# Where in a partition the operands of the matmuls begin: offsets at multiples of 256 and 512 bytes in a hybrid encoder

## The chip, the cores and the metric

The kernel runs on one core of a Trainium2 chip. The metric is the time of one execution on the device, in microseconds. The kernel before was run three times, 2456.8 to 2458.05 us, median 2456.95 us.

## The reference

The trunk has two layers over 16 meta tokens and 256 tokens (272 rows, 2048 features), all in float32. Each layer is a token mixer and a SwiGLU, each behind an RMS norm and added to the residual:

```
h = concatenate(meta, x)                                   # [272, 2048]
layer 0: h += fft2(norm(h), tokens and 256 features).real @ fnet_w_out
         h += (silu(u @ w_gate) * (u @ w_up)) @ w_down     # u = norm(h), 5632 hidden features
layer 1: z, xbc, dt = norm(h) @ ssd_w_in                   # bidirectional state space (SSD) mixer
         y = ssd(silu(conv5(xbc)), dt) forward + backward, 64 heads in 8 groups
         h += group_norm(y * silu(z)) @ ssd_w_out
         h += swiglu(norm(h))
out = norm(h)[16:]
```

## The kernel before

The residual `hT` is held feature-major: 128 partitions, 16 feature blocks, 272 tokens. Every large product is made of three matmuls (`mm3`, L103 to L106): each float32 operand is split in a high and a low part of type float32r, and high·high, high·low and low·high are summed in PSUM. The operands of the activations are `gh`/`gl` (of the normed residual, made by `norm_block`, L142), `hh`/`hl` (of the hidden layer of a SwiGLU), `yh`/`yl` (of the SSD mixer's output) and `fh`/`fl` (of the Fourier mixer). The weights come in units of 1 MB by DMA into `w` (3 buffers); ACT copies each half to `wh` (L97), DVE subtracts to get `wl` (L98), four buffers each. TensorE takes them in this order:

- Fourier mixer, then `fnet_w_out`: weights `wh`/`wl` are the stationary operand, `fh`/`fl` the moving one, 272 columns (to 154 us).
- SwiGLU of layer 0, in pieces of 8 feature blocks: gate and up (`gemm_in`, L115) move `gh`/`gl`, 272 columns; down (`down0`) moves `hh`/`hl`, 272 columns (to 935 us).
- SSD mixer in 8 groups: products with `w_in` move `gh`/`gl` (272 or 258 columns); the gate z turns the roles round and moves `wh`/`wl`, 512 columns, against stationary `gh`/`gl`; small float32 products within a group; `w_out` (`out_group`, L571) moves `yh`/`yl`, 256 columns (to 1706 us).
- Last SwiGLU on the 256 tokens alone: gate and up move `gh`/`gl`, 256 columns; down (`down1`) moves `wh`/`wl`, 512 columns, against stationary `hh`/`hl`.

In `gemm_in` and `down0` each block k of the contraction gives six matmuls in a row that share k: two column blocks j, three products each.

Tiles are placed one behind the other, at multiples of 32 bytes, in the order in which the pools and the tiles in them are made. In the built program `gh` begins at byte 33920 of a partition, `gl` at 51328, `wh` at 98560 and `wl` at 114944 (four buffers of 4096 bytes each), `hh` and `hl` of layer 0 at 134592 and 152000 (8704 bytes each buffer), `yh` and `yl` at 203488 and 211680, `hh` and `hl` of the last SwiGLU at 161280 and 177664. A row (one feature block) of `gh`, `fh` and of layer 0's `hh` has 272 words, 1088 bytes; of `yh` and of the last SwiGLU's `hh` 256 words, 1024 bytes. Modulo 256 the weights thus begin at 0, slices of 128 columns too; rows of 1088 bytes take the offsets 0, 64, 128, 192 by turns; `yh` and `yl` have 224 in every row, the last SwiGLU's `hh` and `hl` 0. In the last SwiGLU gate and up read tokens 16 to 271 of rows of 272.

The schedule is the order in which the code is written, moved by priorities of the splitting (L96); waits come from the tiles' uses.

Of the kernel before, what the change touches and what calls it, by code (L numbers as in the profile page):

```python
# [19 lines left out]
P = 128  # L20
D = 2048
NB = D // P            # 16 feature blocks
NM = 16                # meta tokens
KM = 64 + NM           # rows that hold them three times, from 0, 32 and 64
S = 256
L = NM + S             # 272
FG = 8                 # fnet groups
FD = D // FG           # 256
NK = L // 2 + 1        # 137 token frequencies
# [4 lines left out]
HG = H // G            # heads per group  # L34
NST = 128
DFF = 5632
NF = DFF // P          # 44
EPS = 1e-6
CA = (NM, NM + P)      # token chunk A
CB = (NM + P, L)       # token chunk B  # L40
XC, BC, CC = 0, DI, DI + G * NST      # columns of x, B, C
NRAW, NSP = 3, 4       # buffers: weights as they come (8 KiB a partition), their parts (4 + 4 KiB)
RUN = 1024             # words of a weight block that a partition holds one after the other
HC = 8                 # feature blocks of a piece of the SwiGLU hidden layer
# [4 lines left out]
def encoder(ctx: ExitStack, tc: tile.TileContext, I, out):  # L49
# [4 lines left out]
    wpool = ctx.enter_context(tc.tile_pool(name="wpool", bufs=1))  # L54
    pmm = ctx.enter_context(tc.tile_pool(name="pmm", bufs=4, space=PSUM))
# [16 lines left out]
    rbc = const.tile([P, L], F32, name="rbc")  # L72
    ssq = const.tile([P, L], F32, name="ssq")
# [10 lines left out]
    def weights(src, k0, nk, c0, ncol):  # L84
        """Unit of a weight matrix (see blocks), rows (k0..k0+nk)*128, columns c0..c0+ncol, as (high, low) parts."""
# [16 lines left out]
    def mm3(ps, lhs, rhs, start, stop):  # L102
        """ps (+)= lhs.T @ rhs of operands split as (high, low)."""  # L103
        PE.matmul(ps, lhs[0], rhs[0], start=start, stop=False)  # L104
        PE.matmul(ps, lhs[0], rhs[1], start=False, stop=False)  # L105
        PE.matmul(ps, lhs[1], rhs[0], start=False, stop=stop)  # L106
# [4 lines left out]

    def gsl(k, a, b=L):
        return gh[:, k, a:b], gl[:, k, a:b]

    def gemm_in(src, c0, lo):  # L115
        """Two blocks of 128 columns of norm(h) @ src, feature-major, over the tokens lo.. ."""
        n = L - lo
        pss = [mmtile(), mmtile()]
        for k0 in (0, 8):
            u = weights(src, k0, 8, c0, 256)  # L120
            for k in range(8):
                for j in range(2):
                    mm3(pss[j][:, :n], wsl(u, k, j * P), gsl(k0 + k, lo), k0 + k == 0, k0 + k == NB - 1)
        return pss

    def rsqrt(pool, x, n, tag):
        """1/sqrt(x) of [P, n]: bit-level seed and three Newton steps."""
# [12 lines left out]
    npool = ctx.enter_context(tc.tile_pool(name="npool", bufs=1))  # L140

    def norm_block(b, wcol, lo):  # L142
        """Block b of the residual is final: operand of the next product and sum of squares."""
        SC.activation(gh[:, b, lo:], hT[:, b, lo:], AF.Identity, bias=0.0, scale=wcol)
        V.scalar_tensor_tensor(out=gl[:, b, lo:], in0=hT[:, b, lo:], scalar=wcol,
                               in1=gh[:, b, lo:].bitcast(F32), op0=ALU.mult, op1=ALU.subtract)
# [7 lines left out]
    def norm_scale(lo):  # L154
        """rbc = 1/rms of every token, the same on all partitions."""
        ps = tptile()
        PE.matmul(ps[:, : L - lo], ones, ssq[:, lo:], start=True, stop=True)
        x = npool.tile([P, L], F32, tag="nx", name="nx")
# [16 lines left out]
    # =====================================================================  # L175
    # Fourier mixer
    # =====================================================================
    with ExitStack() as fx:
# [3 lines left out]
        tok = early.tile([P, 2, L], F32, name="tok")  # L182
        tokM = early.tile([KM, L], F32, name="tokM")
# [3 lines left out]
        tm3 = early.tile([KM, L], F32R, name="tm3")  # L187
        th = early.tile([P, 2, L], F32R, name="th")
        tl = early.tile([P, 2, L], F32R, name="tl")
# [4 lines left out]
        # parts of x where the spectrum comes later  # L194
# [49 lines left out]
        def table(c, r):  # L244
            """Token table of chunk c scaled by 1/rms."""
# [4 lines left out]
        with tc.manual_schedule():  # L250
            # residual, feature-major, parts of x, mean squares of the tokens
# [37 lines left out]
            # meta tokens: three products of parts in one, rows 0.. high high, 32.. high low, 64.. low high  # L289
# [8 lines left out]
            # token transform: cosines 0..NK-1, sines 1..NK-2  # L298
# [20 lines left out]
        # feature transform; operands in F32R have an even number of columns, so one more than is used  # L319
# [37 lines left out]
    # =====================================================================  # L357
    # SwiGLU, the hidden layer in pieces of HC feature blocks
    # =====================================================================
    def swiglu(layer, lo, tmp, pieces, down):  # L360
# [3 lines left out]
        for nf in pieces:  # L364
            hh = tmp.tile([P, HC, n], F32R, tag="hh", name="hh", bufs=2)
            hl = tmp.tile([P, HC, n], F32R, tag="hl", name="hl", bufs=2)
# [43 lines left out]
    # =====================================================================  # L410
    # bidirectional SSD mixer
    # =====================================================================
    with ExitStack() as fx:
# [7 lines left out]
        rtok = sc0.tile([P, 2], F32, name="rtok")  # L421
# [3 lines left out]
        sp = fx.enter_context(tc.tile_pool(name="ssd", bufs=1))  # L425

# [9 lines left out]
        # The products with the large weights are emitted in slots; the rest of a group follows its slots at a  # L436
        # distance, so that the tensor engine has a product to go on with meanwhile.
# [12 lines left out]
        def step_sizes():  # L450
# [6 lines left out]
            # 1/rms of the tokens of chunks A and B, one token a partition  # L457
# [14 lines left out]
            # softplus(v) = max(v, 0) + log1p(exp(-|v|)), log1p(t) = 2 atanh(t / (2 + t))  # L472
# [16 lines left out]
            # prefix sums within the chunks: inclusive forward, exclusive backward  # L489
# [42 lines left out]
        def conv(ps, blk, lo, dst):  # L532
            """Depthwise conv over the tokens lo.. of the 128 channels of block blk, then silu."""
            n = L - lo
            u = sp.tile([P, L], F32, tag="cu", name="cu", bufs=2)
            V.tensor_tensor(out=u[:, :n], in0=ps[:, :n], in1=rbc[:, lo:], op=ALU.mult)
            a = sp.tile([P, L], F32, tag="ca", name="ca", bufs=2)
# [10 lines left out]
        def to_tokens(src, dst, dstM):  # L548
            """[128 channels, 272 tokens] -> [tokens, 128 channels] of the chunks A, B and of the meta tokens."""
# [7 lines left out]
        def out_group(gi, q, yh, yl):  # L557
            """Residual += y @ w_out over the channels of group gi, columns 512q.. ."""
# [12 lines left out]
        def group_rest(gi, cT, btok, btokM, xt, xtM, zs, cb):  # L571
            """All of a group after its products with w_in."""
# [5 lines left out]
            def kernels(c):  # L578
                """Within chunk c: sum over both directions of exp(decay) dt B.C, [source, head, target]."""
# [11 lines left out]
            # weighted inputs  # L591
# [24 lines left out]
            sums = sp.tile([P, 2], F32, tag="sums", name="sums", bufs=2)  # L616
            gated = []

            def mix(c):
                """y of chunk c: other chunks' parts, this chunk's part, skip connection; then the gate."""  # L620
# [31 lines left out]
            def norm():  # L652
                """Grouped norm, back to feature-major."""
                V.tensor_scalar(out=sums, in0=sums, scalar1=1.0 / 512, scalar2=EPS, op0=ALU.mult, op1=ALU.add)
                rg = rsqrt(sp, sums, 2, "rg")
                later(1, lambda: back(rg))
# [29 lines left out]
        def decays(gi):  # L686
            """Cumulated log decays of a group's heads on all partitions."""
# [7 lines left out]
        def drop(gi):  # L695
            """The half that a direction doesn't see decays to nothing."""
# [11 lines left out]
        for gi in range(G):  # L708
            if gi % 2 == 0:
# [1 line left out]
                bT = sp.tile([P, 2, L], F32, tag="bT", name="bT", bufs=2)  # L711
                cT = sp.tile([P, 2, S + 2], F32, tag="cT", name="cT", bufs=1)
# [11 lines left out]
            # x of the group  # L724
# [4 lines left out]
            def source_target(gj=gi % 2, cb=cb, bT=bT, cT=cT):  # L729
                """B.C of all sources and targets within the chunks."""  # L730
# [7 lines left out]
            for h2 in range(2):  # L738
                for j, ps in enumerate(gemm_in(I["w_xbc"], XC + gi * 512 + h2 * 256, 0)):
                    bj = 2 * h2 + j  # L740
                    xs = sp.tile([P, L], F32, tag="xs", name="xs", bufs=4)
# [5 lines left out]
            # silu(z) of the group  # L747
# [27 lines left out]
    # =====================================================================  # L775
    # last SwiGLU, final norm
    # =====================================================================
    with ExitStack() as fx:
# [4 lines left out]
        sums = tmp.tile([P, 2, 4], F32, name="fsums")  # L783
        sqj = tmp.tile([P, 512], F32, name="fsq")
        ms = tmp.tile([P, 2], F32, name="fms")

        def down1(f0, nf, hh, hl):
            if f0 == 0:
                # residual, one token a partition
# [59 lines left out]
def tables():  # L849
    """Constants that follow from the shapes."""  # L850
# [20 lines left out]
def blocks(w, ncol):  # L871
    """[.., rows, columns] in blocks [rows of blocks, columns of blocks, 128, (k c)]: RUN words, that is RUN / ncol
    rows 128 apart of ncol columns, one after the other."""
# [6 lines left out]
def arrays_of(inputs):  # L880
    """The matrices in blocks, the per-feature vectors one after the other in rows of 128, the tables."""
# [28 lines left out]
```

## Time and profile before

| | |
|---|---|
| median of the runs | 2456.95 us |
| span of the profiled execution, first to last instruction | 2455.8 us |
| TensorE busy | 2428.0 us, 99% |
| VectorE busy | 1484.5 us, 60% |
| ScalarE busy | 1214.1 us, 49% |
| GpSimd busy | 406.6 us, 17% |
| HBM read over the span | 433.66 MB, 177 GB/s |

The profiled execution is told by its span; what lies around it is the 1.15 us to the median. A row of a group of instructions gives its line, engine, operation, output and inputs, shapes, count, busy time and the mean of one. Matmuls overlap, so that a mean duration is more than what one matmul takes of the span.

### The profile page before, as it was taken

What the parts mean: (1) busy time and instruction counts of PE and PEld (TensorE: products, weight loads), DVE (VectorE), ACT (ScalarE), POOL (GpSimd) and SP (SyncE); (2) the same over time, 40 slices, a digit from 0 to 9 for tenths busy, and PEclk for the clock granted to TensorE, in tenths of its full rate; (3) what the DMA queues carried; (4) which work ended last, traced back from release to release, by engine and by line L of the source; (5) the groups of instructions that cost most, each with busy time, mean ns of one, the idle gap of its engine ahead of it and who ended that gap; (6) DMA issues with size and microseconds to landing.
All of it is one profiled execution on the core that took longest, in us unless ns stands there. A gap on an engine that the chain in (4) does not pass through costs nothing.

```text
span 2455.8 us, 42928 instructions
## 1 busy us (share of the span) xinstructions
PE 2428.0 (99%) x17958; PEld 2316.9 (94%) x17958; DVE 1484.5 (60%) x2020; ACT 1214.1 (49%) x1784; POOL 406.6 (17%) x361
## 2 busy tenths in 40 slices
PE   8999999999999999999999999999999999999998
PEld 8999999999999999888989989989999998989887
DVE  7564545545454568778668668668554555555556
ACT  6444333343434346878557558445444343444434
POOL 3111111010101112232221221112211010102000
PEclk9999999999999999999999999999999999999999
DMA  5555555555555555655455555454555555555553
GB/s 164 175 178 179 173 173 176 181 175 172 175 181 177 172 173 175 213 175 186 164 179 193 177 172 184 159 172 157 201 187 178 189 189 189 189 190 188 189 192 134
DMA packets 115506, 438.66 MB, mean 179 GB/s; under 512 B 7360, under 2 KB 8080, under 8 KB 115136
## 3 DMA queue, kind: packets, MB, share of 16 engines
q1 hardware_dynamic: 110336, 417.86, 50.4%
q0 software_dynamic: 4832, 17.99, 2.3%
q8 instruction: 141, 2.31, 0.4%
q14 instruction: 53, 0.43, 0.0%
q10 hardware_dynamic: 144, 0.07, 0.0%
HBM read 433.66 MB, written 2.23 MB: 177 GB/s over the span
## 4 chain that ended last, share of the span: by engine, by line
PE 89%; DVE 3%; DMA 3%; issue 2%; ACT 2%; POOL 1%; SPq 0%; DVEq 0%; ACTq 0%; POOLq 0%
PE mm L105 29%; PE mm L106 28%; PE mm L104 28%; DMA pb<-scr 2%; DVE wl L98 1%; PE tp L642 1%; ACT wh L97 1%; DVE ca L544 1%; PE tp L626 0%; PE tp L665 0%; DMA w<-fnet_w_out 0%; POOL pb L701 0%; ACT pb L584 0%; DMA x<-x 0%; PE tp L608 0%
## 5 line engine op out<-in xcount | busy, mean ns | idle before, releaser
L98 DVE TENSOR_TENSOR wl<-w,wh 128x1024 fp32r<-128x1024 f32 x786 | 970.0, 1236 | 840.7 <-ACT wh L97 832.7
L97 ACT CAST wh<-w 128x1024 fp32r<-128x1024 f32 x786 | 822.8, 1048 | 1096.6 <-PE mm L105 809.2
L105 PE MATMUL mm<-gl,wh 128*128 128x272 f32 (+2 forms) x3600 | 1026.0, 285 | 0.0
L106 PE MATMUL mm<-gh,wl 128*128 128x272 f32 (+2 forms) x3600 | 1022.3, 284 | 0.5 <-DVE wl L98 0.5
L104 PE MATMUL mm<-gh,wh 128*128 128x272 f32 (+2 forms) x3600 | 1022.4, 284 | 0.1
L104 PEld LDWEIGHTS mm<-gh,wh 128*128 128x128 f32 x3600 | 678.2, 188 | 1.1 <-issue 0.5
L106 PEld LDWEIGHTS mm<-gh,wl 128*128 128x128 f32 x3600 | 676.3, 188 | 0.9 <-DVE wl L98 0.7
L105 PEld LDWEIGHTS mm<-gl,wh 128*128 128x128 f32 x3600 | 676.1, 188 | 0.8 <-issue 0.5
L378 POOL TENSOR_TENSOR s<-s,rbc 128x272 f32<-128x272 f32 (+1 forms) x88 | 96.4, 1113 | 816.4 <-ACT s L377 816.4
L105 PE MATMUL mm<-hl,wh 128*128 128x272 f32 x704 | 203.7, 289 | 0.0
L106 PE MATMUL mm<-hh,wl 128*128 128x272 f32 x704 | 202.7, 288 | 0.0
L104 PE MATMUL mm<-hh,wh 128*128 128x272 f32 x704 | 200.9, 285 | 0.0
L385 POOL TENSOR_TENSOR hl<-t,hh 128x272 fp32r<-128x272 f32 (+1 forms) x88 | 97.0, 1121 | 397.1 <-ACT hh L384 397.1
L104 PE MATMUL mm<-yh,wh 128*128 128x256 f32 x512 | 146.5, 288 | 3.8 <-DVE hT L567 3.3
L105 PE MATMUL mm<-yl,wh 128*128 128x256 f32 x512 | 143.6, 281 | 0.5 <-DVE yl L671 0.5
L106 PE MATMUL mm<-yh,wl 128*128 128x256 f32 x512 | 143.5, 281 | 0.0
L105 PE MATMUL mm<-wl,hh 128*128 128x512 f32 x352 | 137.1, 390 | 0.0
L104 PE MATMUL mm<-wh,hh 128*128 128x512 f32 x352 | 137.0, 389 | 0.0
L106 PE MATMUL mm<-wh,hl 128*128 128x512 f32 x352 | 137.0, 389 | 0.0
L104 PEld LDWEIGHTS mm<-hh,wh 128*128 128x128 f32 x704 | 132.9, 189 | 0.0
L106 PEld LDWEIGHTS mm<-hh,wl 128*128 128x128 f32 x704 | 132.3, 188 | 0.0
L105 PEld LDWEIGHTS mm<-hl,wh 128*128 128x128 f32 x704 | 132.1, 188 | 0.0
(279 smaller groups left out, 2858.5 us busy)
## 6 DMA issues: line engine op xcount, KB each, us to landing
w<-ffn_w_gate SPq DMA_DIRECT2D x88, 1024.0 KB, 5.1
w<-ffn_w_up SPq DMA_DIRECT2D x88, 1024.0 KB, 5.1
w<-w_down SPq DMA_DIRECT2D x80, 1024.0 KB, 5.1
w<-w_xbc SPq DMA_DIRECT2D x48, 1024.0 KB, 5.2
w<-w_z SPq DMA_DIRECT2D x32, 1024.0 KB, 5.3
w<-ssd_w_out SPq DMA_DIRECT2D x32, 1024.0 KB, 5.1
w<-fnet_w_out SPq DMA_DIRECT2D x16, 1024.0 KB, 5.1
pb<-scr POOLq DMA_DIRECT2D x32, 512.0 KB, 5.6
```

The lines of the kernel that those rows point to most:

```text
L97: SC.copy(wh, w[:, ks, :])
L98: V.tensor_tensor(out=wl, in0=w[:, ks, :], in1=wh.bitcast(F32), op=ALU.subtract)
L104: PE.matmul(ps, lhs[0], rhs[0], start=start, stop=False)
L105: PE.matmul(ps, lhs[0], rhs[1], start=False, stop=False)
L106: PE.matmul(ps, lhs[1], rhs[0], start=False, stop=stop)
L378: GP.tensor_tensor(out=s1, in0=s1, in1=rbc[:, lo:], op=ALU.mult)
L385: GP.tensor_tensor(out=hl[:, f, :], in0=t2, in1=hh[:, f, :].bitcast(F32), op=ALU.subtract)
L544: V.scalar_tensor_tensor(out=a[:, o0:o1], in0=u[:, i0 : i0 + o1 - o0], scalar=w(j), in1=a[:, o0:o1], op0=ALU.mult, op1=ALU.add)
L642: PE.matmul(py[:, e * HD : (e + 1) * HD], kern[c][:, e, :], xt[:, c, e * HD : (e + 1) * HD], start=True, stop=True)
```

## The change

Tiles are placed otherwise, and two of them are laid out otherwise:

- A pad of 384 bytes ahead of `hT` brings `hT`, `gh`, `gl`, `ident`, `ones` and `cols` to multiples of 512 bytes; `rbc` and `ssq` go to the norm's pool, which now stands behind the weights' pool and has its own pad. `w`, `wh` and `wl` so begin at multiples of 512 too (`wh` at 96768).
- In the pools of the Fourier mixer and the SSD mixer the tiles that TensorE reads most come first; those of 272 columns or of a few words go to the end or to a pool of their own (`so`).
- `hh`/`hl` of layer 0's SwiGLU get rows of 320 words (1280 bytes), of which 272 are used. All their rows, and all of `yh`/`yl`, begin at 0 modulo 256.
- For tokens 16 to 271 (the last SwiGLU's input) `norm_block` writes and `gemm_in` reads a compact view of `gh`/`gl`: 16 rows of 256 words from the tile's start, 1024 bytes apart.
- `nx` shares the buffer of `sq`; the final norm's small tiles share one of 512 bytes.

The instructions and their order are the same on all five engines, but for the names of tiles.

```diff
+    npool = ctx.enter_context(tc.tile_pool(name="npool", bufs=1))
...
+    const.tile([P, LINE - 32], F32, name="pad")
     hT = const.tile([P, NB, L], F32, name="hT")
     gh = const.tile([P, NB, L], F32R, name="gh")
     gl = const.tile([P, NB, L], F32R, name="gl")
...
-    rbc = const.tile([P, L], F32, name="rbc")
-    ssq = const.tile([P, L], F32, name="ssq")
...
+    gh1, gl1 = (x.rearrange("p b t -> p (b t)")[:, : NB * S].rearrange("p (b t) -> p b t", t=S) for x in (gh, gl))
+
     def gsl(k, a, b=L):
+        if (a, b) == (NM, L):
+            return gh1[:, k, :], gl1[:, k, :]
         return gh[:, k, a:b], gl[:, k, a:b]
...
+    rbc = npool.tile([P, L], F32, name="rbc")
+    ssq = npool.tile([P, L], F32, name="ssq")
+
+    npool.tile([P, L], F32, tag="sq", name="sq", bufs=1)
+    npool.tile([P, L], I32, tag="nyi", name="nyi")
+    npool.tile([P, LINE // 2], F32, name="pad2")
...
     def norm_block(b, wcol, lo):
-        SC.activation(gh[:, b, lo:], hT[:, b, lo:], AF.Identity, bias=0.0, scale=wcol)
-        V.scalar_tensor_tensor(out=gl[:, b, lo:], in0=hT[:, b, lo:], scalar=wcol,
-                               in1=gh[:, b, lo:].bitcast(F32), op0=ALU.mult, op1=ALU.subtract)
+        high, low = gsl(b, lo)
+        SC.activation(high, hT[:, b, lo:], AF.Identity, bias=0.0, scale=wcol)
+        V.scalar_tensor_tensor(out=low, in0=hT[:, b, lo:], scalar=wcol,
+                               in1=high.bitcast(F32), op0=ALU.mult, op1=ALU.subtract)
...
-        x = npool.tile([P, L], F32, tag="nx", name="nx")
+        x = npool.tile([P, L], F32, tag="sq", name="nx", bufs=1)
...
-            hh = tmp.tile([P, HC, n], F32R, tag="hh", name="hh", bufs=2)
-            hl = tmp.tile([P, HC, n], F32R, tag="hl", name="hl", bufs=2)
+            hh = tmp.tile([P, HC, n + -n % 64], F32R, tag="hh", name="hh", bufs=2)[:, :, :n]
+            hl = tmp.tile([P, HC, n + -n % 64], F32R, tag="hl", name="hl", bufs=2)[:, :, :n]
...
         sp = fx.enter_context(tc.tile_pool(name="ssd", bufs=1))
+        so = fx.enter_context(tc.tile_pool(name="ssdo", bufs=1))
...
-            u = sp.tile([P, L], F32, tag="cu", name="cu", bufs=2)
+            u = so.tile([P, L], F32, tag="cu", name="cu", bufs=2)
...
-                bT = sp.tile([P, 2, L], F32, tag="bT", name="bT", bufs=2)
-                cT = sp.tile([P, 2, S + 2], F32, tag="cT", name="cT", bufs=1)
+                bT = so.tile([P, 2, L], F32, tag="bT", name="bT", bufs=2)
+                cT = so.tile([P, 2, S + 2], F32, tag="cT", name="cT", bufs=1)
```

## Rows read from the trace of the kernel before

**Rows 1.** The page's head and parts 1 and 2: span, busy time, granted clock

```profile
span 2455.8 us, 42928 instructions
PE 2428.0 (99%) x17958; PEld 2316.9 (94%) x17958; DVE 1484.5 (60%) x2020; ACT 1214.1 (49%) x1784; POOL 406.6 (17%) x361
PEclk9999999999999999999999999999999999999999
```

**Rows 2.** The page's part 4, the chain by line

```profile
PE mm L105 29%; PE mm L106 28%; PE mm L104 28%; DMA pb<-scr 2%; DVE wl L98 1%; PE tp L642 1%; ACT wh L97 1%; DVE ca L544 1%; PE tp L626 0%; PE tp L665 0%; DMA w<-fnet_w_out 0%; POOL pb L701 0%; ACT pb L584 0%; DMA x<-x 0%; PE tp L608 0%
```

**Rows 3.** Who TensorE waited for: us in total, times, longest us

```profile
PE tp L225 <- DMA ident<-c_ident: 5.2, 1, 5.2
PE mm L104 <- DVE hT L567: 3.3, 4, 1.6
```

**Rows 4.** Groups of instructions by shape: count, busy us, mean ns, idle before

```profile
L104 PE MATMUL mm<-gh,wh 128*128 128x272 f32 x2064 | 591.2, 287 | 0.0
L104 PE MATMUL mm<-gh,wh 128*128 128x256 f32 x1408 | 394.5, 280 | 0.1
L105 PE MATMUL mm<-hl,wh 128*128 128x272 f32 x704 | 203.7, 289 | 0.0
L104 PE MATMUL mm<-yh,wh 128*128 128x256 f32 x512 | 146.5, 288 | 3.8 <-DVE hT L567 3.3 <-ACT yh L670 0.5
L104 PE MATMUL mm<-wh,hh 128*128 128x512 f32 x352 | 137.0, 389 | 0.0
L104 PE MATMUL mm<-wh,gh 128*128 128x512 f32 x256 | 101.6, 397 | 0.0
```

**Rows 5.** Stretches of one kind of matmul, busy us and count by engine

```profile
core 0: us, PE busy (x) PEld busy (x) DVE busy (x) ACT busy (x) POOL busy (x), PEclk, DMA share, GB/s
160.00:280.00 120.00, 120.00 (x963) 120.00 (x962) 60.11 (x68) 50.41 (x63) 24.49 (x22) 1.00 0.49 166
841.00:931.00 90.00, 90.00 (x722) 90.00 (x721) 57.10 (x73) 41.46 (x57) 11.96 (x14) 1.00 0.53 176
1000.00:1016.00 16.00, 16.00 (x71) 12.99 (x70) 13.13 (x14) 14.23 (x27) 1.44 (x2) 1.00 0.61 206
1684.00:1696.00 12.00, 12.00 (x104) 12.00 (x103) 10.38 (x19) 8.11 (x17) 6.16 (x5) 1.00 0.40 145
1720.00:1880.00 160.00, 160.00 (x1370) 160.00 (x1369) 84.91 (x99) 69.23 (x87) 32.57 (x30) 1.00 0.57 190
1893.00:1933.00 40.00, 40.00 (x178) 33.15 (x177) 21.18 (x21) 15.82 (x15) 0.00 (x0) 1.00 0.49 162
```

**Rows 6.** TensorE in order of time: start us, duration, a run at offset 0

```profile
start us, us, engine line op out<-in xcount [idle before <-releaser]
2002.20 0.27 PE L105 MATMUL mm<-gl,wh 128*128 128x256 f32 x1
2002.32 0.28 PE L106 MATMUL mm<-gh,wl 128*128 128x256 f32 x1
2002.43 0.28 PE L104 MATMUL mm<-gh,wh 128*128 128x256 f32 x1
2002.55 0.28 PE L105 MATMUL mm<-gl,wh 128*128 128x256 f32 x1
2002.67 0.28 PE L106 MATMUL mm<-gh,wl 128*128 128x256 f32 x1
```

**Rows 7.** The same, end of a run at offset 192

```profile
2004.44 0.28 PE L106 MATMUL mm<-gh,wl 128*128 128x256 f32 x1
2004.55 0.28 PE L104 MATMUL mm<-gh,wh 128*128 128x256 f32 x1
2004.66 0.28 PE L105 MATMUL mm<-gl,wh 128*128 128x256 f32 x1
2004.78 0.28 PE L106 MATMUL mm<-gh,wl 128*128 128x256 f32 x1
```

**Rows 8.** Groups by shape again, the SSD mixer's largest small product

```profile
L642 PEld LDWEIGHTS tp<-xt,pb 128*128 128x128 f32 x256 | 31.1, 192 | 7.7 <-issue 6.9 <-PE mm L106 0.5 <-DVE cu L536 0.2
```

More of the change, by code (lines that the diff above doesn't have):

```diff
@@ L43 @@
 RUN = 1024
+LINE = 128
 HC = 8
@@ L138, in rsqrt @@
         return y
-    npool = ctx.enter_context(tc.tile_pool(name="npool", bufs=1))
+    rbc = npool.tile([P, L], F32, name="rbc")
[3 more added lines that the diff above has]
+    npool.tile([P, LINE // 2], F32, name="pad2")
     def norm_block(b, wcol, lo):
-        SC.activation(gh[:, b, lo:], hT[:, b, lo:], AF.Identity, bias=0.0, scale=wcol)
-        V.scalar_tensor_tensor(out=gl[:, b, lo:], in0=hT[:, b, lo:], scalar=wcol,
-                               in1=gh[:, b, lo:].bitcast(F32), op0=ALU.mult, op1=ALU.subtract)
+        high, low = gsl(b, lo)
+        SC.activation(high, hT[:, b, lo:], AF.Identity, bias=0.0, scale=wcol)
+        V.scalar_tensor_tensor(out=low, in0=hT[:, b, lo:], scalar=wcol,
+                               in1=high.bitcast(F32), op0=ALU.mult, op1=ALU.subtract)
         if b == 0:
@@ L181, in encoder @@
         xm = early.tile([KM, D], F32, name="xm")
-        tok = early.tile([P, 2, L], F32, name="tok")
-        tokM = early.tile([KM, L], F32, name="tokM")
         feat = early.tile([P, 2, 2, FD], F32, name="feat")
@@ L186, in encoder @@
         xm3 = early.tile([KM, D], F32R, name="xm3")
-        tm3 = early.tile([KM, L], F32R, name="tm3")
-        th = early.tile([P, 2, L], F32R, name="th")
-        tl = early.tile([P, 2, L], F32R, name="tl")
         fth = early.tile([P, 2, 2, FD], F32R, name="fth")
@@ L193, in encoder @@
         fl = early.tile([P, NB, L], F32R, name="fl")
+        tok = early.tile([P, 2, L], F32, name="tok")
+        tokM = early.tile([KM, L], F32, name="tokM")
+        tm3 = early.tile([KM, L], F32R, name="tm3")
+        th = early.tile([P, 2, L], F32R, name="th")
+        tl = early.tile([P, 2, L], F32R, name="tl")
         xh = fh.rearrange("p b t -> p (b t)")[:, : 2 * D].rearrange("p (c d) -> p c d", c=2)
@@ L420, in encoder @@
         dsk = sc0.tile([P, H], F32, name="dsk")
-        rtok = sc0.tile([P, 2], F32, name="rtok")
+        rtok = sc0.tile([P, 2 + 2 * 8], F32, name="rtok")[:, 0:2]
         scr = dram.tile([P, 2 * P], F32, name="scr")
@@ L534, in conv @@
             n = L - lo
-            u = sp.tile([P, L], F32, tag="cu", name="cu", bufs=2)
+            u = so.tile([P, L], F32, tag="cu", name="cu", bufs=2)
             V.tensor_tensor(out=u[:, :n], in0=ps[:, :n], in1=rbc[:, lo:], op=ALU.mult)
-            a = sp.tile([P, L], F32, tag="ca", name="ca", bufs=2)
+            a = so.tile([P, L], F32, tag="ca", name="ca", bufs=2)
             def w(j):
@@ L614, in states @@
                 SC.copy(st[:, 2, :], ps)
-            sums = sp.tile([P, 2], F32, tag="sums", name="sums", bufs=2)
+            sums = so.tile([P, 2], F32, tag="sums", name="sums", bufs=2)
             gated = []
@@ L654, in norm @@
                 V.tensor_scalar(out=sums, in0=sums, scalar1=1.0 / 512, scalar2=EPS, op0=ALU.mult, op1=ALU.add)
-                rg = rsqrt(sp, sums, 2, "rg")
+                rg = rsqrt(so, sums, 2, "rg")
                 later(1, lambda: back(rg))
@@ L740, in encoder @@
                     bj = 2 * h2 + j
-                    xs = sp.tile([P, L], F32, tag="xs", name="xs", bufs=4)
+                    xs = so.tile([P, L], F32, tag="xs", name="xs", bufs=4)
                     conv(ps, 4 * gi + bj, 0, xs)
@@ L782, in encoder @@
         GP.dma_start(fw, I["norm_final_w"].partition_broadcast(P))
-        sums = tmp.tile([P, 2, 4], F32, name="fsums")
         sqj = tmp.tile([P, 512], F32, name="fsq")
-        ms = tmp.tile([P, 2], F32, name="fms")
+        small = tmp.tile([P, LINE], F32, name="fsmall")
+        sums = small[:, 0:8].rearrange("p (c q) -> p c q", c=2)
+        ms = small[:, 8:10]
         def down1(f0, nf, hh, hl):
```

## The prediction

> **What bounds the kernel now.** I read the page's first two parts, then the chain, then TensorE's waits, then the groups of matmuls, and last a table of stretches. TensorE is busy 2428.0 of 2455.8 us, at the full granted clock from end to end [rows 1], and 85% of the chain are the three matmul lines L104 to L106 [rows 2]. What TensorE waits for is small: the longest waits are 5.2 us for the first transfer and 3.3 us behind L567 [rows 3]. So only the pace of the matmuls can move the time by much. The order of instructions doesn't move: on all five engines the changed program has the same rows in the same order, names aside, and two waits fewer, both on DVE. The change is one of addresses alone.
>
> The pace is not read from the duration of one matmul (280 to 397 ns, [rows 4]), since matmuls overlap; it is the distance from start to start. In a stretch that holds one kind only, that is (length of the stretch + one duration) / count. From [rows 5], with durations from [rows 4]:
> - gate and up of layer 0, 272 columns: (120 + 0.287) / 963 = 124.9 ns
> - down of layer 0, 272 columns: (90 + 0.289) / 722 = 125.05 ns
> - the gate z, 512 columns: (16 + 0.397) / 71 = 230.9 ns
> - `w_out`, 256 columns: (12 + 0.288) / 104 = 118.2 ns
> - gate and up of the last SwiGLU, 256 columns: (160 + 0.280) / 1370 = 117.0 ns
> - down of the last SwiGLU, 512 columns: (40 + 0.389) / 178 = 226.9 ns
>
> Two of these have the same shape and the full clock [rows 5], and differ: 230.9 against 226.9 ns at 512 columns. Their moving operand is the same buffer (`wh`, `wl`); the stationary one is `gh`/`gl` with rows of 1088 bytes in the first, `hh`/`hl` with rows of 1024 bytes in the second. In both, the load of the next weights runs beside the matmul (PEld is busy in the same stretch, [rows 5]). So where the two reads lie to one another costs TensorE time. At 226.9 / 512 = 0.443 ns a column the even stretch is also the quickest per column of the six: the others come to 0.451 to 0.462.
>
> I count offsets modulo 256 bytes: in the even stretch the moving tiles begin at 256 and the stationary ones at 0 modulo 512, and it is even all the same. That 0 against 0, which it will be afterwards, runs alike is an assumption; if not, 1056 matmuls times 4.0 ns = +4.2 us.
>
> **The change part by part.** Modulo 256 nothing changes where rows stay 1088 bytes apart, since four rows in turn take the offsets 0, 64, 128 and 192 wherever the tile begins: Fourier output, gate and up of layer 0, all products with `w_in`, z. I cost these at 0. Three families change.
>
> Gate and up of the last SwiGLU (3 x 1408 = 4224 matmuls): the compact rows of 1024 bytes put every moving operand at offset 0 against weights at 0, where they cycle through four offsets now. At the rate of the even stretch one takes 256 x 0.443 = 113.4 ns, so 4224 x (117.0 - 113.4) = -15.2 us. Each k of a unit makes six matmuls in a row at one offset, and k is counted from the unit's start. The trace has this pace at 256 columns already: at the end of the run of six with offset 192 the starts go 2004.44, 2004.55, 2004.66, 2004.78, that is 0.34 / 3 = 113 ns [rows 7]. Against it stands the run of six with offset 0, from 2002.20 to 2002.67 0.47 / 4 = 117.5 ns, and its last two steps are 0.12 each [rows 6]. A run of six may still carry the offsets before it, the even stretch has hundreds in a row; so I take 113.4, and keep 120 as the upper bound.
>
> `w_out` (3 x 512 = 1536 matmuls): `yh` and `yl` lie at 224 modulo 256 now, all rows alike, and will lie at 0. A single offset is thus not enough for the good pace (118.2 ns). The same 113.4 gives 1536 x (113.4 - 118.2) = -7.4 us; its row has only 104 matmuls, so this term is good to about 1.5 us.
>
> Down of layer 0 (3 x 704 = 2112 matmuls): rows of 1280 instead of 1088 bytes, all at offset 0, but each operand has 1088 bytes, so the next one doesn't begin where this one ends, as it does with 1024. No row shows this. Bounds: the even rate gives 272 x 0.443 = 120.5 ns, 2112 x -4.55 = -9.6 us; the 120 ns of above, 6.6 over the even 113.4, put on 120.5 gives 127.1, +4.3 us. I take 0, between them and at the row of today.
>
> The small products of the SSD mixer (`xt`, `pb`, `xw`, `st`, `dg`): the largest group is L642, 256 weight loads of 192 ns, 31.1 us in all [rows 8]; a tenth of that either way would be 3 us, I take 0. On ACT, DVE and POOL the same operations stand with the same element counts; moved buffers make no new wait, and where the last SwiGLU now overlies `yh` and `yl`, its first writes come behind products that follow the readers on TensorE anyway. That a quicker TensorE is fed: in the stretch of gate and up DVE is busy 84.91, ACT 69.23 of 160 us and the DMA engines 0.57 [rows 5], so 3% more pace has its cover; without it the 15.2 us would not come.
>
> Sum: -15.2 - 7.4 + 0 = -22.6 us. The profiled span is 2455.8 us and the median of the runs 2456.95, so 1.15 us lie around the span and are not touched: 2456.95 - 22.6 = 2434.4 us (2434.35).
>
> A sentence of the Trainium skill speaks against all this: TensorE: Matmul & The Clock Gate (section Step-by-step: what each phase is for) says that TensorE has two independent read ports, so that loading the next weights takes no read bandwidth from the running matmul, and SBUF — State Buffer (Operand start alignment) calls where an operand starts a matter of legality, not of speed, though it timed nothing. By that the two stretches of 512 columns would run alike; they differ by 4.0 ns, so the trace does not agree. That page of the Trainium skill gives for matmuls back to back (section Back-to-back issue gap) columns / 2.4 + 2.5 ns, which would be 215.8 ns at 512 and 109.2 at 256 columns; no stretch here reaches it, the measured pace goes into the sum.
>
> **The rivals.**
> 1. A fixed offset of 0 is no better than the mix. For it: the run at offset 0 makes 117.5 ns [rows 6], and `w_out` with a fixed offset makes 118.2. Against it: the even 512. Price: 4224 x (117.5 - 117.0) - 1536 x (118.2 - 117.5) = +2.1 - 1.1 = +1.0 us, 2458; by 118.2 for both +5.1 us, 2462; a pace of 116 gives -4.2 - 3.4 = -7.6, 2449.4.
> 2. It is slower: at 256 columns a matmul and the load beside it meet in the same place at every step, because both begin at 0 and nothing shifts them. At 512 the second half of a matmul has no load beside it, in which it can get clear; at 256 there is no such half. For it: the run at offset 0 gets slower towards its end, 0.12 and 0.12 [rows 6]. Against it: the same pair of offsets in the even stretch. Price at 120 ns: 4224 x 3.0 + 1536 x 1.8 + 4.3 = 12.7 + 2.8 + 4.3 = +19.8 us, 2476.8. It decides from the point where the pace at offset 0 is over 117.3 ns: there the two large terms cancel.
> 3. Offsets don't matter, and the 4 ns at 512 columns come from the other work beside them (z has ACT busy 14.23 of 16 us, the even stretch 15.82 of 40): 2457. The two ports of the Trainium skill (TensorE: Matmul & The Clock Gate, section Step-by-step: what each phase is for) would make this of it.
>
> **How the numbers follow.** A measurement of this kernel can tell about 0.2%, 4.9 us, from no change. Forecast 0.48: 2434.4, its own range 2420 to 2443 (down of layer 0 at its lower or upper bound, with 3 us of the small products and 1.5 us of `w_out`). Rival 1 0.25, spread over 2449 to 2463: 0.06 faster, 0.12 same, 0.07 slower. Rival 2 0.20. Rival 3 0.07, same. Together 0.54 faster, 0.19 same, 0.27 slower. The range for 8 in 10 goes from 2422 to 2474: nearly all of the forecast, rivals 1 and 3 whole, the milder part of rival 2.
>
> **What would show it.** In the changed profile the stretch of gate and up in the last SwiGLU has one start each 113.4 ns (1413 in 160 us instead of 1370), `w_out` likewise, down of layer 0 between 120.5 and 127, and gate and up of layer 0 still 124.9, z 230.9, the last down 226.9. The waits of TensorE stay as short as now. If gate and up keep 117 or go to 120, the forecast is wrong at its first term; if a family that I left at 0 moves, offsets count otherwise than modulo 256; if waits of TensorE for L98 grow, the quicker pace was not fed.

## The result, and the profile after

The changed kernel takes 2472.51 us (median; 2471.03 to 2473.42) against 2457.4 for the kernel before in the same comparison (2456.8 to 2458.05): ratio 1.0061, 95% interval 1.0047 to 1.0076. It is slower by 15.1 us. The forecast was 2434.4 us, so its sign was wrong; the slower rival's price was 2476.8.

The head of the page after shows that hardly anything but TensorE's own pace has changed [rows 1]:

```profile
span 2470.8 us, 42926 instructions
PE 2443.7 (99%) x17958; PEld 2333.9 (94%) x17958; DVE 1484.2 (60%) x2020; ACT 1213.7 (49%) x1784; POOL 404.6 (16%) x361
PEclk9999999999999999999999999999999999999999
```

The span grew by 15.0 us and TensorE's busy time by 15.7, with the same 17958 matmuls. Away from the two ends of the span the granted clock is the same but for one place: from 1106.7 to 1110.1 us it was 0.50, the lower of its two levels (1.2 GHz), after TensorE had waited 1.70 us for L569. The sixteen matmuls there took 3.39 us against 2.07 before, so about 1.3 of the 15.0 us are the clock's; none of the families that the change touches ran then. The busy times of DVE, ACT and POOL moved by 2 us or less. The chain still runs over the three matmul lines (L105 to L107 now, [rows 2]), and TensorE's waits are as short as before [rows 3]:

```profile
PE mm L106 30%; PE mm L107 29%; PE mm L105 29%; DVE wl L99 1%; PE tp L656 1%; DMA pb<-scr 1%; ACT wh L98 1%; PE tp L679 0%; PE tp L640 0%; DMA w<-fnet_w_out 0%; DVE ca L558 0%; PE tp L622 0%; PE tp L619 0%; ACT pb L598 0%; PE tp L627 0%
```

```profile
PE mm L105 <- DVE hT L581: 3.9, 4, 1.9
```

The stretches that answer to [rows 5], of the kernel after (later stages begin up to 15 us later, so the windows are shifted). The columns are the window in us, then busy us and, in brackets, the count of instructions on each engine, TensorE's granted clock, the DMA share, and GB/s:

```profile
160.00:280.00 120.00, 120.00 (x962) 120.00 (x962) 58.81 (x65) 50.33 (x64) 24.55 (x22) 1.00 0.48 163
842.00:932.00 90.00, 90.00 (x720) 90.00 (x719) 58.48 (x74) 41.40 (x59) 11.59 (x13) 1.00 0.51 175
1000.00:1016.00 16.00, 16.00 (x71) 12.99 (x70) 12.79 (x12) 13.65 (x25) 3.31 (x3) 1.00 0.63 222
1178.00:1188.00 10.00, 10.00 (x86) 10.00 (x85) 4.77 (x9) 3.15 (x3) 0.00 (x0) 1.00 0.43 136
1724.00:1884.00 160.00, 160.00 (x1335) 160.00 (x1335) 82.73 (x94) 67.74 (x86) 30.71 (x29) 1.00 0.55 185
1900.00:1940.00 40.00, 40.00 (x178) 33.15 (x177) 21.02 (x21) 15.82 (x15) 0.00 (x0) 1.00 0.47 163
```

By the prediction's formula (stretch plus one duration, over the count), gate and up of the last SwiGLU, the fifth row, went from 1370 starts to 1335: (160 + 0.283) / 1335 = 120.06 ns instead of 117.0. Layer 0's gate and up (125.0), z (230.9) and the last down (226.9) stand where they stood, and layer 0's down moved little (90.29 / 720 = 125.4). The fourth row, `w_out`, is short: 10.28 / 86 = 119.5, good to about 1%. Within the stretch of gate and up, matmul follows matmul (columns: start us, duration):

```profile
2002.00 0.28 PE L105 MATMUL mm<-gh,wh 128*128 128x256 f32 x1
2002.12 0.28 PE L106 MATMUL mm<-gl,wh 128*128 128x256 f32 x1
2002.24 0.28 PE L107 MATMUL mm<-gh,wl 128*128 128x256 f32 x1
2002.36 0.28 PE L105 MATMUL mm<-gh,wh 128*128 128x256 f32 x1
```

Each step is 0.12 us. The last two steps of [rows 6] were the same 0.12; [rows 7] had 0.34 / 3 = 0.113.

For exact sums I added the distances from each matmul's start to the next one's in both traces, family by family:

| family | matmuls | before, us | after, us | difference |
|---|---|---|---|---|
| gate and up, last SwiGLU, 256 columns | 4224 | 494.4 | 507.1 | +12.7 |
| `w_out`, 256 columns, its waits included | 1536 | 190.9 | 193.7 | +2.8 |
| down of layer 0, 272 columns | 2112 | 264.0 | 264.7 | +0.7 |
| gate and up of layer 0 and products with `w_in`, 272 columns | 6192 | 781.1 | 781.4 | +0.3 |
| last down, 512 columns | 1056 | 239.8 | 239.8 | 0 |
| z, 512 columns | 768 | 181.1 | 180.7 | -0.4 |
| small products of the SSD mixer | 734 | 116.0 | 115.2 | -0.8 |

The first three rows are +16.2 us and the others take about 1 back (the 1.3 us of the slower clock are in the fourth and the last row). The largest row, +12.7 us, is the family that reads the compact view.

### The profile page after: what moved, and what is told of

It reads as the page before. It is cut to its first block, busy times and chain, and to the rows that moved or that the text cites. A ratio compares the mean times of both kernels' runs of the same rounds, so it can differ in the third digit from the quotient of the medians.

```text
span 2470.8 us, 42926 instructions
## 1 busy us (share of the span) xinstructions
PE 2443.7 (99%) x17958; PEld 2333.9 (94%) x17958; DVE 1484.2 (60%) x2020; ACT 1213.7 (49%) x1784; POOL 404.6 (16%) x361
## 4 chain that ended last, share of the span: by engine, by line
PE 92%; DVE 3%; ACT 1%; DMA 1%; issue 1%; POOL 0%; SPq 0%; DVEq 0%; ACTq 0%; POOLq 0%
PE mm L106 30%; PE mm L107 29%; PE mm L105 29%; DVE wl L99 1%; PE tp L656 1%; DMA pb<-scr 1%; ACT wh L98 1%; PE tp L679 0%; PE tp L640 0%; DMA w<-fnet_w_out 0%; DVE ca L558 0%; PE tp L622 0%; PE tp L619 0%; ACT pb L598 0%; PE tp L627 0%
## 5 line engine op out<-in xcount | busy, mean ns | idle before, releaser
L107 PE MATMUL mm<-gh,wl 128*128 128x272 f32 (+2 forms) x3600 | 1029.6, 286 | 0.5 <-DVE wl L99 0.5
L105 PE MATMUL mm<-gh,wh 128*128 128x272 f32 (+2 forms) x3600 | 1027.1, 285 | 0.0
L105 PEld LDWEIGHTS mm<-gh,wh 128*128 128x128 f32 x3600 | 684.4, 190 | 1.1 <-issue 0.7
L107 PEld LDWEIGHTS mm<-gh,wl 128*128 128x128 f32 x3600 | 682.4, 190 | 0.9 <-DVE wl L99 0.7
L107 PE MATMUL mm<-hh,wl 128*128 128x272 f32 x704 | 202.4, 288 | 0.0
L105 PE MATMUL mm<-hh,wh 128*128 128x272 f32 x704 | 202.4, 287 | 0.0
L105 PE MATMUL mm<-yh,wh 128*128 128x256 f32 x512 | 147.4, 290 | 4.4 <-DVE hT L581 3.9
L107 PE MATMUL mm<-yh,wl 128*128 128x256 f32 x512 | 144.5, 283 | 0.0
L105 PE MATMUL mm<-wh,hh 128*128 128x512 f32 x352 | 137.1, 389 | 0.0
L107 PE MATMUL mm<-wh,hl 128*128 128x512 f32 x352 | 136.9, 389 | 0.0
L105 PEld LDWEIGHTS mm<-hh,wh 128*128 128x128 f32 x704 | 132.4, 188 | 0.0
L107 PEld LDWEIGHTS mm<-hh,wl 128*128 128x128 f32 x704 | 132.3, 188 | 0.0
```

## The experiments

All numbers on offsets below are modulo 256 bytes. "192 on 0" means that the moving operand begins at 192 and the stationary one at 0. In the changed kernel everything in the three families is 0 on 0. The kernels differ from the changed one in addresses alone.

**Another single offset.** All three families at 192 on 0:

```diff
-    ... [:, : NB * S] ... for x in (gh, gl))
+    ... [:, 48 : 48 + NB * S] ... for x in (gh, gl))
+            if gi == 0:
+                sp.tile([P, 48], F32, name="ypad")
...
-            hh = ... [:, :, :n]
+            hh = ... [:, :, 48 : 48 + n]      # layer 0; hl alike
```

> The changed kernel, but the compact gh and gl, yh and yl, and the rows of layer 0's hh and hl all begin at 192 modulo 256 instead of 0; the weights stay at 0. Theory 1 (the offset of the moving operand to the weights sets the pace, and 0 is a bad one at 256 columns): gate and up of the last SwiGLU and w_out go at 113.4 ns a matmul, as the end of the run at offset 192 in the kernel before did, instead of 120.0; that is (4224 + 1536) x -6.6 = -38 us against the changed kernel, about 2434.5 us; the 272 columns of layer 0's down between 120.5 and 125. Theory 2 (rows that never shift against the weights are bad at any offset): 118 to 120 ns stay, 2465 to 2473 us. Theory 3 (it is not the offset but the layout in rows of 1024 bytes): 120 ns stay in gate and up, 2472 us.

Measured: 2452.68 us, ratio to the kernel before 0.9978 (0.9969 to 0.9987). Its trace has two paces at the same shape and the same offsets. The rows are down of layer 0, two stretches of `w_out`, and gate and up:

```profile
842.00:928.00 86.00, 86.00 (x699) 86.00 (x698) 56.32 (x71) 40.65 (x58) 11.47 (x13) 1.00 0.50 173
1159.00:1168.00 9.00, 9.00 (x82) 9.00 (x81) 7.84 (x15) 8.05 (x19) 5.60 (x5) 1.00 0.43 142
1172.00:1182.00 10.00, 10.00 (x87) 10.00 (x86) 5.16 (x9) 2.92 (x4) 0.27 (x1) 1.00 0.42 125
1712.00:1872.00 160.00, 160.00 (x1361) 160.00 (x1360) 83.94 (x96) 69.07 (x87) 32.60 (x30) 1.00 0.55 188
```

`w_out` runs at 9.28 / 82 = 113 ns in one stretch and at 10.28 / 87 = 118 in the next. From start to start (the mean distance of neighbouring starts, from the second tenth of a stretch on) it is 113.3 and 117.8, each held to the end of the stretch. The six stretches behind the mixer's 512-column products (`xw`, `btok`) have 117.8, six behind 128-column ones (`dg`, `yg` or `ident`, `xs`) 113.3. Gate and up have 113.3 in their first 96 matmuls and 160.28 / 1361 = 117.8 in all that follow. So the offset matters (120 became 117.8), down of layer 0 gained 1.9 ns (123.45), and the 113 ns that the forecast counted on exist. But the offset alone does not give them. The program may not either: nine of this kernel's ten runs lie between 2451.31 and 2453.81 us, one took 2445.89. The first long stretch of gate and up, 1440 matmuls, at 113.3 instead of 117.8 would take 6.5 us less (an estimate from the two paces); that run has no trace, so this is not shown.

**The compact view taken back**, the rest of the change kept:

```diff
     def gsl(k, a, b=L):
-        if (a, b) == (NM, L):
-            return gh1[:, k, :], gl1[:, k, :]
         return gh[:, k, a:b], gl[:, k, a:b]
```

> The changed kernel without the compact view: in the last SwiGLU gh and gl keep rows of 1088 bytes, everything else as changed. Theories 1, 2 and 3 alike: gate and up go back from 120.0 to 117.0 ns, 4224 x -3.0 = -12.7 us, about 2460 us, and what is left of the loss (2 to 3 us) is w_out, still at 120 ns. If gate and up stay at 120 the other moved tiles did it, and all three theories fall.

Measured: 2459.3 us, ratio 1.0006 (0.9997 to 1.0016), no difference that can be told. Gate and up are back at 117.0 (160.28 / 1371 = 116.9), `w_out` is still at 120.0 from start to start:

```profile
1724.00:1884.00 160.00, 160.00 (x1371) 160.00 (x1370) 83.64 (x94) 69.19 (x87) 32.54 (x30) 1.00 0.55 190
```

The kernel is 13.2 us quicker than the changed one. That settles which edit costs the time: the view, which fixes at 0 what had cycled through four offsets.

**Sweeps over offsets**, one run each. The same edits as in the first experiment, with 64 and 224 for gate and up, 128 and 32 for `w_out`, and another offset in each piece of layer 0's hidden layer:

> The changed kernel with other offsets, to read paces by stretch: compact gh and gl at 64, yh and yl at 128, the six pieces of layer 0's hh and hl at 32, 32, 64, 96, 128 and 160 bytes. Theory 1: gate and up about 117.6 ns (the run at 64 of the kernel before), w_out about 117 (the run at 128), the pieces at 272 columns differ from each other by several ns between 120.5 and 128. Theory 2: all at 256 columns 118 to 120 ns, all pieces alike. Theory 3: gate and up at 120, w_out at 118 to 120.

> As the sweep before, with the compact gh and gl at 224, yh and yl at 32, the six pieces of layer 0's hh and hl at 0, 16, 48, 80, 112 and 144 bytes. Theory 1: gate and up at 118.2 ns, which is what w_out had in the kernel before at the same offset of 224 (one offset, one pace, whichever the tile); w_out at 32 has no row, anything from 113 to 121; piece 0 at 125.3 as in the changed kernel. Theory 2: 118 to 120 everywhere. Theory 3: gate and up stay at 120.

Measured: 2463.73 and 2459.59 us. Gate and up at 64 and at 224, the first run and then the second:

```profile
1724.00:1884.00 160.00, 160.00 (x1361) 160.00 (x1360) 83.94 (x96) 69.06 (x87) 32.59 (x30) 1.00 0.55 187
```

```profile
1724.00:1884.00 160.00, 160.00 (x1354) 160.00 (x1353) 80.19 (x86) 68.28 (x87) 32.52 (x30) 1.00 0.55 186
```

With the paces from start to start, over both runs, the first one, and for `w_out` at 160 the run entered from 0 below:

| moving offset, on weights at 0 | 256 columns, ns | 272 columns, ns |
|---|---|---|
| 0 | 120.0 | 125.3 |
| 16 / 32 / 48 | - / 116.7 / - | 124.4 / 125.7 / 125.0 |
| 64 | 117.8 | 126.7 |
| 80 / 96 / 112 | - | 125.0 / 126.7 / 126.7 |
| 128 | 118.7 or 120.0 | 126.7 |
| 144 / 160 | - / 117.3 or 118.7 | 124.4 / 123.4 |
| 192 | 117.8 or 113.3 | 123.3 |
| 224 | 118.3 | - |
| four in turn | 117.0 | 125.0 |

Each offset has its pace or pair of paces, 0 is the slowest at 256 columns (128 comes to the same 120.0 in five of its fifteen stretches, all five behind `xw`, `btok`), and no offset reached 113 by itself but 192. Theories by which offsets don't matter, or by which any single offset costs 118 to 120, fall (32 gives 116.7).

**How 192 is entered.** In the kernel before, runs at 192 followed runs at 128. So block 0 was set to 128 and blocks 1 to 15 to 192, and in a second kernel to 0 and 192. Both also move the hidden layer of the last SwiGLU, which is the stationary operand at 512 columns, and have offsets of their own in `w_out` (192, then 160) and in down of layer 0 (160, then its high and low parts at different ones), which the lines below do not show:

```diff
     def gsl(k, a, b=L):
         if (a, b) == (NM, L):
-            return gh1[:, k, :], gl1[:, k, :]
+            o = 48 + k * S if k else 32       # second kernel: else 0
+            return flat[0][:, o : o + S], flat[1][:, o : o + S]
```

> Changed kernel with other offsets. Last SwiGLU's gate/up: block 0 of the 16 begins at offset 128, blocks 1 to 15 at 192, so that every unit enters the run at 192 from 128, as the kernel before did. w_out at 192, down of layer 0 at 160, hidden layer of the last SwiGLU (stationary side, 512 columns) at 192. Theory A (192 has two paces, 117.7 and 113.4, and what came before decides): gate/up near 113.6, so 4224 x 4.1 = -17 us against the run with 192 alone, where it stayed at 117.7. Theory B (one offset, one pace): gate/up stays at 117.5 to 117.8. w_out 115.8 by both, down of layer 0 123.4. The 512-column down: if an offset matters only when it changes from matmul to matmul (as between the stationary blocks of gate z, 230.9), 226.7 stays; if the stationary offset itself matters, it moves, between 220 and 236. Time by A with 226.7: 2452.7 - 17 = 2436; by B 2453.

> As the run before in this call, but block 0 of the last SwiGLU's gate/up at offset 0 and blocks 1 to 15 at 192: the run at 192 is entered from 0. Theory A (what came before decides): a pace of its own, 113.5 if any change of offset does it, 117.7 if only the step from 128 does. Theory B: 117.5 to 117.9. w_out at 160: 115 to 117.5. Down of layer 0 with high and low part at different offsets (192/160, 160/192, 192/128, 128/192, 192/64, 64/192 in its six pieces): if a change of offset from matmul to matmul costs something, 124 to 127; if the mean of the single offsets holds, 123.4, 123.4, 124.4, 125.5, 124.5, 125.6. Hidden layer of the last SwiGLU at 64: 226.7 if the stationary side's own offset does not matter.

Measured, entered from 128: 2443.9 us, ratio 0.9947 (0.9931 to 0.9964). Two stretches of gate and up, then the 512-column down (hidden layer at 192):

```profile
1712.00:1872.00 160.00, 160.00 (x1360) 160.00 (x1359) 83.87 (x95) 68.59 (x87) 32.69 (x30) 1.00 0.54 187
1930.00:2010.00 80.00, 80.00 (x706) 80.00 (x705) 41.37 (x44) 35.08 (x44) 15.21 (x14) 1.00 0.57 197
1886.00:1925.00 39.00, 39.00 (x172) 32.02 (x171) 20.93 (x21) 15.10 (x15) 0.00 (x0) 1.00 0.48 164
```

One kernel, one family, one list of offsets: 113.5 ns in the first 96 matmuls, 160.28 / 1360 = 117.9 through the next 1440, with fifteen steps from 128 into 192 among them, and 80.28 / 706 = 113.7 in the 768 after the first down. Entered from 0 (2447.36 us, a single run; gate and up, then the down with its hidden layer at 64):

```profile
1716.00:1876.00 160.00, 160.00 (x1409) 160.00 (x1408) 86.97 (x100) 70.59 (x89) 32.70 (x30) 1.00 0.57 197
1888.00:1926.00 38.00, 38.00 (x164) 30.64 (x163) 19.86 (x20) 14.73 (x14) 0.00 (x0) 1.00 0.47 171
```

160.28 / 1409 = 113.75, and 113.3 to 113.7 in all seven stretches. So what came before a run, and not its offset alone, decides which of two paces it keeps, as theory A has it. A step from 0 reached the quick pace each time, one from 128 only sometimes. The stationary operand's own offset matters at 512 columns: 226.7 became 228.9 (at 192) and 233.3 (at 64). These runs lost 2.2 and 6.8 us there.

**The weights moved instead.** All weight parts begin at 192 (a 192-byte tile ahead of them, the pad behind cut by as much):

```diff
+    wpool.tile([P, 48], F32, name="wpad")
...
-    npool.tile([P, LINE // 2], F32, name="pad2")
+    npool.tile([P, LINE // 2 - 48], F32, name="pad2")
...
```

> Changed kernel with all weight parts moved by 192 bytes: they are the stationary operand of the 256- and 272-column families and the moving operand of the 512-column ones. Gate/up of the last SwiGLU keeps its tokens at 0, w_out's at 192, down of layer 0 at 0, 0, 64, 128, 192, 192 in its six pieces. Theory C (the distance between moving and stationary start decides): w_out (192 on 192) as 0 on 0, so 120; gate/up (0 on 192) as 64 on 0, so 117.8; down of layer 0 125.3 at 192 on 192, 126.7 at 0 on 192. Theory D (only the moving operand's own offset decides): gate/up 120, w_out 115.8, down of layer 0 125.3, 125.3, 126.7, 126.7, 123.3, 123.3; the 512-column down, whose moving operand now begins at 192, leaves 226.7.

Measured: 2471.06 us in one run. Down of layer 0 in four windows (moving at 0, 64, 128 and 192), `w_out` (192), gate and up (0), and the 512-column down (192 on 0):

```profile
410.00:450.00 40.00, 40.00 (x318) 40.00 (x317) 22.21 (x28) 13.64 (x13) 0.00 (x0) 1.00 0.51 180
552.00:596.00 44.00, 44.00 (x349) 44.00 (x348) 23.42 (x29) 14.86 (x15) 1.89 (x2) 1.00 0.49 168
698.00:740.00 42.00, 42.00 (x343) 42.00 (x342) 22.85 (x28) 15.28 (x15) 0.55 (x1) 1.00 0.52 178
842.00:932.00 90.00, 90.00 (x720) 90.00 (x719) 58.32 (x74) 41.40 (x59) 11.26 (x13) 1.00 0.50 176
1178.00:1187.00 9.00, 9.00 (x77) 9.00 (x76) 4.53 (x8) 2.61 (x3) 0.00 (x0) 1.00 0.38 123
1724.00:1884.00 160.00, 160.00 (x1361) 160.00 (x1360) 83.90 (x96) 69.22 (x87) 32.52 (x30) 1.00 0.54 188
1900.00:1938.00 38.00, 38.00 (x164) 30.62 (x163) 20.19 (x20) 14.12 (x14) 0.00 (x0) 1.00 0.47 166
```

This is the run that names the quantity. It is the distance from the stationary operand's start to the moving one's, modulo 256 (0 on 192 counts as 64):

| pair | distance | measured, ns | same distance on weights at 0 |
|---|---|---|---|
| 256 columns, 192 on 192 | 0 | 120.0 (start to start) | 120.0 |
| 256 columns, 0 on 192 | 64 | 160.28 / 1361 = 117.8 | 117.8 |
| 272 columns, 0 on 192 | 64 | 40.29 / 318 = 126.7 | 126.7 |
| 272 columns, 64 on 192 | 128 | 44.29 / 349 = 126.9 | 126.7 |
| 272 columns, 128 on 192 | 192 | 42.29 / 343 = 123.3 | 123.3 |
| 272 columns, 192 on 192 | 0 | 90.29 / 720 = 125.4 | 125.3 |
| 512 columns, 192 on 0 | 192 | 233.3 (start to start) | 233.3 (0 on 64) |

The distance holds in all of them, as theory C has it; theory D (the moving offset alone) is wrong in five of the seven.

**Different offsets for the high and the low part** (moving offsets alternate 192, 128, 192 within a product):

> Changed kernel with the high part of the last SwiGLU's tokens at 192 and the low part at 128, so that the moving offset alternates 192, 128, 192 within each product. If a change of offset from matmul to matmul throws the pair into the faster pace (theory A): 113.5 to 115.5; if paces only average (theory B): (117.7 x 2 + 119.1) / 3 = 118.2; 4224 matmuls, so 11 to 20 us between them. Down of layer 0, high/low at 192/0, 0/192, 160/128, 176/176, 144/176, 176/160: by averages 124.0, 124.7, 124.5, 123.4 to 124.5 for the rest. Hidden layer of the last SwiGLU at 128 on the stationary side: 226.7 if its own offset does not matter. w_out at 0 as in the changed kernel: 120.

Measured: 2472.29 us in one run; gate and up at 118.75 (160.28 / 1350), near the average of the single offsets; the 512-column down at 232.3 with its hidden layer at 128:

```profile
1724.00:1884.00 160.00, 160.00 (x1350) 160.00 (x1349) 82.74 (x93) 68.09 (x86) 32.51 (x30) 1.00 0.53 185
```

So alternating offsets did not reach the quick pace. Down of layer 0 with its two parts at different offsets gave 124.4 to 125.6 here and 124.4 to 126.6 in the run entered from 0, and with 0/192 128.9, 4 ns over the average of 124.7: a mix is not the mean of its offsets either.

**Putting it together.** The same list (block 0 at 0, the rest at 192) for gate and up and for `w_out`, down of layer 0 at 192, the hidden layer of the last SwiGLU left at 0 on 0; beside it the one edit of gate and up alone, and the mirror (block 0 at 192, the rest at 0):

```diff
...
+            yh, yl = ([t[:, 48 + k * S if k else 0 :][:, :S] for k in range(4)] for t in
+                      (sp.tile([P, 4 * S + 64], F32R, tag=x, name=x, bufs=2) for x in ("yh", "yl")))
...
```

> Changed kernel with, for gate/up of the last SwiGLU and for w_out, the first block of every product at offset 0 and the others at 192; down of layer 0 at 192; hidden layer of the last SwiGLU left at 0. If the step from 0 into 192 always ends in the faster pace: gate/up 480.9 us as in the run that entered from 0 (changed kernel 507.1, -26.2), w_out 1504 x (120.0 - 113.8) = -9.3, down of layer 0 264.7 - 260.5 = -4.2; 2472.5 - 39.7 = 2432.8. If w_out, whose run at 192 lasts only 18 of 24 matmuls, falls back to 117.7: 2438.

> Changed kernel with one edit: gate/up of the last SwiGLU begins at offset 0 in block 0 and at 192 in blocks 1 to 15. If the pace of this family alone carries the change's loss: 507.1 - 480.9 = 26.2 us less than the changed kernel, 2446.3 (2443 to 2449), w_out at 120 and down of layer 0 at 125.3 as before. If something else of the change costs time too, more than that is left over.

> Changed kernel with the mirror of that: gate/up of the last SwiGLU has block 0 at 192 and blocks 1 to 15 at 0. If offset 0 also has a faster pace that a start from elsewhere reaches: under 117; if 0 has the one pace: 119.5 to 120.1. w_out at 64: 117.8. Down of layer 0 with its first block at another offset than the rest, 0/192, 0/192, 64/192, 128/192, 0/160, 0/144 in its six pieces: if 272 columns have a faster pace as well, 120 to 122; otherwise 123.4 to 124.5, as with one offset.

Measured, all three families: 2434.67 us (2434.58 to 2435.33), ratio to the kernel before 0.9909 (0.9894 to 0.9925). Page head; gate and up of layer 0, down of layer 0, `w_out`, gate and up of the last SwiGLU, last down:

```profile
span 2432.7 us, 42926 instructions
```

```profile
160.00:280.00 120.00, 120.00 (x962) 120.00 (x961) 58.52 (x64) 50.33 (x64) 24.51 (x22) 1.00 0.48 163
842.00:928.00 86.00, 86.00 (x699) 86.00 (x699) 56.23 (x71) 40.78 (x57) 12.03 (x13) 1.00 0.51 174
1173.00:1182.00 9.00, 9.00 (x81) 9.00 (x80) 4.45 (x8) 3.16 (x3) 0.00 (x0) 1.00 0.38 128
1712.00:1872.00 160.00, 160.00 (x1409) 160.00 (x1408) 86.19 (x96) 70.78 (x89) 32.69 (x30) 1.00 0.57 194
1880.00:1918.00 38.00, 38.00 (x169) 31.47 (x168) 20.74 (x20) 14.73 (x15) 0.00 (x0) 1.00 0.47 166
```

From start to start: gate and up 480.8 us (-26.3 against the changed kernel), `w_out` 186.9 (-6.8), down of layer 0 260.5 (-4.2), the last down unchanged. These 37.3 us are nearly all of the 37.8 between the two medians. `w_out` gained less than the -9.3 expected: each product is six matmuls at 0 (117.9 on average), six at 192 that still settle (115.9) and only twelve at 113.5, together 115.2.

Gate and up alone: 2445.36 us, ratio 0.9954 (0.9941 to 0.9966), 27.2 us under the changed kernel where 26.2 were expected; gate and up at 160.28 / 1409 = 113.75. The mirror, one run: 2464.42 us, gate and up at 160.28 / 1341 = 119.5. At distance 0 no quicker pace appeared in the places where a step led into it. Down of layer 0 with a first block elsewhere and the rest at 192 came to 123.75 to 124.4, no better than 123.3 with one offset. The one edit, then the mirror:

```profile
1724.00:1884.00 160.00, 160.00 (x1409) 160.00 (x1408) 86.18 (x97) 71.36 (x89) 32.70 (x30) 1.00 0.56 194
1724.00:1884.00 160.00, 160.00 (x1341) 160.00 (x1340) 79.59 (x84) 67.26 (x87) 32.55 (x30) 1.00 0.54 184
```

## Why the prediction was wrong

- **Right: what bounds the kernel.** Only TensorE's pace moved, waits stayed short, and the quicker kernels were fed: at 113.75 ns in gate and up DVE was busy 86.19 and ACT 70.78 of 160 us.
- **Right: which families move.** Offsets count modulo 256 and the families with rows of 1088 bytes stand still (+0.3 and -0.4 us). The one assumption named there, that 0 on 0 at 512 columns runs like today's even stretch, held (226.9).
- **Wrong: "At the rate of the even stretch one takes 256 x 0.443 = 113.4 ns".** This is the step that failed. It carries what 0 on 0 measured at 512 columns over to 256, as a price per column. Measured at distance 0 are 226.7 ns at 512 columns and 120.0 at 256, 6.6 more than the 113.4. What doesn't carry is the rank of the offset: distance 0 is the best of the four measured at 512 columns and the slowest at 256. The even stretch is also cheap per column because it is long: a line through 226.7 and 120.0 has 0.417 ns a column and 13.3 ns for each matmul (an estimate; at 272 columns the line gives 126.7, measured are 125.3). A fixed part read from the rows of before would not have helped: the two mixed stretches, 230.9 and 117.0, give 0.445 ns a column, and 226.9 less 256 of these is 113.0. So the term of gate and up was 4224 x (120.06 - 117.0) = +12.9 instead of -15.2, and the term of `w_out` +2.8 instead of -7.4.
- **Wrong in its weight: the two steps of 0.12 us.** [rows 6] showed the pace of a settled run at offset 0, and they were kept only as an upper bound, because "a run of six may still carry the offsets before it". It does, and that speaks the other way round: the 113 ns of [rows 7] were no sign of offset 0, they belong to 192 and to what precedes it there. Averaged over all runs of six in that family of the trace before, the last three steps are 118.4, 119.2 and 120.8 ns at 0, and 113.5 each at 192.
- **Right by its bounds: down of layer 0.** 0 taken, +0.7 measured, the bounds were -9.6 and +4.3.
- **Rival 2 came about in its place and nearly at its price**: 12.7 + 2.8, as it said, and 0.7 in place of 4.3. The measured time lies inside the range of 2422 to 2474 only because that took in part of this rival; the forecast's own range ended at 2443. Its image (both begin at 0, so every step meets the last one's load in the same place) is borne out in one part: 192 on 192 is as slow as 0 on 0, so it is the common start that counts, not the address 0. Its second part, why 512 columns don't suffer, stays open: at 512 columns distance 0 is the best of the four measured (226.7 against 228.9, 232.3 and 233.3), and the rows show no free half there, since the load is busy 33.15 of the 40 us [rows 5].
- **Rival 3 falls.** Addresses alone move 256 columns between 113.3 and 120.0 ns and 512 columns between 226.7 and 233.3. The Trainium skill (TensorE: Matmul & The Clock Gate, section Step-by-step: what each phase is for) says that loading the next weights takes no SBUF read bandwidth from the running matmul. The runs don't agree that the two reads leave one another alone, since the distance between them sets the pace; whether bandwidth is what they share, no run shows. The formula that the prediction takes from the same page of the Trainium skill (section Back-to-back issue gap) is given there for a matmul by itself and said to miscount a stream with a weight load to each matmul, so that no stretch reaches it says nothing against that section.

What stays open: why one run at 192 settles at 113.3 and the next at 117.8. The runs show that what precedes goes with it, and that a step from 0 led to the quick pace in every stretch of gate and up; they don't show what state is kept. By what mechanism the distance acts is open too: no run takes the weight load away, so its part in it is argued from the distance alone.

## What to carry to other kernels

Where TensorE is the bound and each matmul has its own weight load beside it, as here, the distance between the starts of the two operands modulo 256 bytes was worth some 6% of the pace at 256 columns and 3% at 512, and aligning both to the same round number was the slowest choice at 256 columns and the best measured at 512. Measure the pace (count of starts in a stretch of one kind) for each width on its own: neither a price per column nor the rank of an offset carried from one width to the other here. A uniform layout also takes away a mix in which some runs are quick: before making offsets uniform, look at what each of them does in the mix, averaged over many runs.

## What the runs showed of the hardware

- The pace of back-to-back matmuls with their own weight loads depends on (moving start - stationary start) modulo 256 bytes: at 256 columns 120.0 ns at 0, 116.7 at 32, 117.8 at 64, 118.7 or 120.0 at 128, 117.3 or 118.7 at 160, 113.3 or 117.8 at 192, 118.3 at 224; at 512 columns 226.7 at 0, 228.9 at 64, 232.3 at 128, 233.3 at 192.
- At 256 columns and distance 192 a run kept the pace that it fell into for up to 1440 matmuls. In one kernel both paces occurred, and a first block at 0 led to the quicker in every stretch of gate and up.
- At 272 columns the paces lie between 123.3 (192) and 126.7 (64, 96, 112 and 128), with 125.3 at 0; a step into 192 from elsewhere brought nothing there.
